# Eight projection tiles of layer 1 as plain F32 matmuls in a two-layer decoder trunk

## The chip, the cores and the metric

The kernel runs on one core of one Trainium2 chip. The metric is the device time of one execution in microseconds; of three runs the median was 1395.73 us (1391.5 to 1395.9). The engines are PE (TensorE: PE for matmuls, PEld for the weight loads beside them), DVE (VectorE), ACT (ScalarE), POOL (GpSimd) and SP (SyncE, from which the DMAs of this kernel are issued). Each engine works off its own instructions in a fixed order.

## The reference, cut to what matters

The input x has 512 tokens of width 1024, all in float32, and there are two layers. Each layer normalises x, multiplies it by one wide matrix `w_in`, and gives the columns of the product to three groups of heads: low-rank latent attention (cq, ckv, kr), sparse attention with an indexer that picks the 128 best keys of each query (aq, ak, av, qi, ki, wi), and retention (rq, rk, rv, rg).

```
for l in range(DEPTH):
    h = rmsnorm(x, g_mix[l])
    (cq, ckv, kr, aq, ak, av, qi, ki, wi, rq, rk, rv, rg) = jnp.split(h @ w_in[l], split_at, axis=-1)
    ...                       # three groups of heads
    x = x + jnp.concatenate([o_a, o_b, o_c], axis=-1) @ w_out[l]
    hf = rmsnorm(x, g_mlp[l])
    x = x + jnp.square(jax.nn.relu(hf @ w_ff1[l])) @ w_ff2[l]
return rmsnorm(x, g_final)
```

The change concerns the product `h @ w_in` of the first layer.

## The kernel before, in words

The activations lie transposed, features on the 128 partitions and the 512 tokens along a row, so x is eight tiles of 128x512. `w_in` is worked in tiles of 128 output columns: tile n (`win[l, n]`, 128x1024 in memory) holds the eight 128x128 blocks for the eight x tiles. Tile 0 feeds the latent key, 1 and 2 are the index queries qi0 and qi1, 3 and 4 the retention queries rq0 and rq1, 5 and 6 the retention keys rk0 and rk1, 7 and 8 the gates rg0 and rg1, 9 and 10 the sparse queries aq0 and aq1, 11 and 12 kv, 13 to 18 the latent queries cq0 to cq5. Columns that are needed with tokens on the partitions are worked apart ("tk", the token tiles, L677 to L707).

A product keeps float32 accuracy by halves. `make_u` (L281) writes x times the gain as a high half in fp32r and a low half, the difference. `wsplit` (L199) does the same with a weight tile: two 128x512 copies into `wh` (L187 on ACT, or L189 on POOL) and two subtractions into `wl` (L209 on DVE, or L211 on POOL). `product` (L215) then runs, for each of the eight blocks, `mm3` (L143): high by high, high by low, low by high, thus 24 fp32r matmuls of 128x512 for a tile. The norm's factor is applied to the product afterwards (`scaled`, L642).

Which engine makes the halves turns with a counter by `MHI = 'aaap'` and `MLO = 'vp'`: three copies in four on ACT, the subtractions in turn on DVE and POOL. Raw weight tiles have `WRB = 4` buffers (`wr`), halves `WB = 4` each. Tiles of the general pool `g` have 13 buffers.

The order of the tiles in a layer is written out in the string `ORDER`: after qi0, rg0, qi1 and the token tiles ("tk") it goes through rq0, rk0, rq1, rk1, rg1, aq1, aq0, kv0, kv1 and cq0 to cq5, with index scores ("ix", L715), top-k rounds ("t", L731) and retention scores ("r", L781) between. A list scheduler sets the place of every instruction on its engine, by the priorities in `PRI`; a top-k round has -225, so it fills what is left of DVE. A round finds the eight largest scores of a row (L734) and strikes them out (L735); there are 48 rounds in a layer, and three masks (L739) behind them.

A rotary tile (rq, rk, aq, qi) is scaled on DVE, its halves are swapped by two DMAs (L302), and the tables (L291, DMA) are multiplied in on POOL and DVE (L138); `rq_tile` (L759) then splits it and sends the halves by DMA into the `qk` tiles (L768, L769). Index scores go through a relu on ACT (L722) and are summed on DVE (L727). The retention scores multiply the `qk` tiles of rq and rk.

For the latent queries `factor` (L882) makes a norm factor out of summed squares: a chain of small DVE instructions from L247 to L887. `round_rope` (L952) and L976 apply it to the query products.

Of the kernel before, what the change touches and what calls it, by code (L numbers as in the profile page):

```python
# [11 lines left out]
FR = mybir.dt.float32r  # L12
BF = mybir.dt.bfloat16
AF = mybir.ActivationFunctionType
ALU = mybir.AluOpType
AX = mybir.AxisListType

P = 128
# [3 lines left out]
KD = 8  # L22
# [8 lines left out]
WRB = 4  # L31
# [24 lines left out]
MLO = 'vp'  # L56
ORDER = 'qi0 rg0 qi1 tk ix1 ix2 F rq0 ix3 rk0 rq1 r1 t2 r1 r1 t3 rk1 t4 rg1 aq1 r1 r1 aq0 F t2 t2 F F F F F t2 F F kv0 kv1 F F t1 F F r2 cq0 t2 t2 r1 r1 cq1 r4 kvf kvc t2 cq2 cq3 t5 r7 cq4 t1 t4 r16 t4 t2 cq5 r12 F F r6 r12 t1 F r2 v0 r16 r14 F r14 r9 cqf r2 t4 mk F t2 r1 r2 cqc r2 r2 r3 F t1 r11 rr0 t1 t4 t4 q0 r4 k1 t5 F k0 t2 r4 F t2 r2 q1 t4 r6 t4 r2 F t10 t10 t3 t4 m0 r2 r6 t2 r5 m1 r3 r2 r1 t3 t2 t5 a0 a1 t2 k2 t4 t4 dm t7 t4 r10 r1 t9 rr1 r1 t7 t3 r2 t4 a2 q2 a3 q3 t3 r3 m2 r7 t6 r10 r2 d2 t5 d3 d0 t15 d1 k3 t4 t2 r2 t2 t1 t3 m3 v1 a4 t8 t1 a6 F t3 r2 t4 t59 t2 r1 t6 r2 a7 r2 t3 t1 t3 a5 t2 t3 F r1 F r3 r2 r10 F r2 F'
PRI = {'fin': 0, 'w': 99, 'e': 59, 't': -225, 'rope': 0, 'split': 133, 'q': -16, 'qm': 0, 'rr': 0, 'v': 5, 'k': 0, 'att': 0, 'pv': 0, 'done': -70, 'ret': -44, 'st': 65, 'x': 0, 'tab': -20, 'cq': 0, 'tok': 15, 'idx': 0, 'dm': 8, 'rg': 0, 'km': 0, 'qi': 0, 'aq': 0}
TOPK = 128
NEG = -1e30  # L60
GONE = -3e38
# [4 lines left out]
G_MIX, G_MLP, G_Q, G_KV, G_RET, G_LAYER = 0, 8, 16, 22, 24, 26  # L66
# [5 lines left out]
def trunk_kernel(ctx, tc, xT, gains, win, wtk, wuq, wukv, wout, wff1, wff2, tabs, cf, cb, outT):  # L72
    nc = tc.nc
# [9 lines left out]
    def hp(k):  # L83
        return tc.high_priority(PRI[k]) if PRI[k] else nullcontext()

    def nm(s):
        count["n"] += 1
        return f"{s}_{count['n']}"

    def S(tag, bufs, shape=None, dt=F32):  # L90
        return sb.tile(shape or [P, T], dt, tag=tag, bufs=bufs, name=nm(tag))

    def g_(dt=F32, shape=None):
        return S("g", GB, shape, dt)
# [3 lines left out]
    def pair(tag, bufs, dt=FR):  # L98
        t = S(tag, bufs, [P, 2, T], dt)
        return t[:, 0], t[:, 1]  # L100

    def x_():
        if not spare:
            spare.extend(pair("x", 4, F32))
        return spare.pop(0)
# [16 lines left out]
    def tiny(w, tag="tiny", bufs=8, dt=F32):  # L122
        return sb.tile([P, w], dt, tag=tag, bufs=bufs, name=nm(tag))

    def mm_ps():
        return pp.tile([P, T], F32, tag="mm", bufs=3, name=nm("mm"))
# [13 lines left out]
    def mm(out, lhsT, rhs, start, stop):  # L140
        return nc.tensor.matmul(out, lhsT, rhs, start=start, stop=stop)  # L141

    def mm3(out, ah, al, bh, bl, start, stop):  # L143
        mm(out, ah, bh, start, False)
        mm(out, ah, bl, False, False)
        return mm(out, al, bh, False, stop)
# [12 lines left out]
    x = [x_() for k in range(KD)]  # L159
# [20 lines left out]
    def gcol(i):  # L180
        return gn[:, i : i + 1]
# [11 lines left out]
    def wchunk(src, width, parts=2):  # L193
        with hp("w"):
            raw = S("wr", WRB, [P, 1024])[:, :width]
            nc.sync.dma_start(raw, src)
            return wsplit(raw, width, parts)

    def wsplit(raw, width, parts):  # L199
        res = []  # L200
        w = width // parts
        for c in range(parts):
            hi, lo = S("wh", WB, None, FR)[:, :w], S("wl", WB, None, FR)[:, :w]
            rc = raw[:, c * w : (c + 1) * w]
            n = count["w"]
            count["w"] += 1
            copy_fr(hi, rc, H0[n] if n < len(H0) else mode["hi"][n % len(mode["hi"])])
            if (L0[n] if n < len(L0) else mode["lo"][n % len(mode["lo"])]) == "v":
                nc.vector.tensor_sub(lo, rc, R(hi))  # L209
            else:  # L210
                nc.gpsimd.tensor_sub(lo, rc, R(hi))  # L211
            res.append((hi, lo))
        return res

    def product(ch, kk, acts, cols=slice(0, T), out=None):  # L215
        out = mm_ps() if out is None else out
        per = len(kk) // len(ch)
        for j, k in enumerate(kk):
            ah, al = acts[k]
            h, l = ch[j // per]  # L220
            js = slice(j % per * P, j % per * P + P)
            order[j] = mm3(out[:, cols], h[:, js], l[:, js], ah[:, cols], al[:, cols], j == 0, j == len(kk) - 1)
        return out

    def gemm(wsrc, kk, acts, raw=None):
        parts = 2 if len(kk) > 2 else 1
        ch = wchunk(wsrc, len(kk) * P, parts) if raw is None else wsplit(raw, len(kk) * P, parts)
        return product(ch, kk, acts)
# [25 lines left out]
    def stats(ss, dim, r2=None):  # L254
        with hp("st"):
            ps = sc_ps()
            for b in range(NB):
                mm(ps[:, b : b + 1], ss[:, b * P : (b + 1) * P], ones, True, True)
            return rstd(ps[:, :4], dim, r2)

    def bcast(y, out):
        with hp("st"):
            ps = sc_ps()
            for b in range(NB):
                nc.tensor.transpose(ps[:, b * P : (b + 1) * P], y[:, b : b + 1].to_broadcast([P, P]), ident)
            nc.scalar.activation(out, ps, AF.Copy)
# [11 lines left out]
    def after(key):  # L278
        return tc.issue_after(order[key].ins) if key in order else nullcontext()

    def make_u(xk, gc):  # L281
        uh, ul = u2()
        order["uh"] = nc.scalar.activation(uh, xk, AF.Copy, scale=gc)
        order["ul"] = nc.vector.scalar_tensor_tensor(ul, xk, gc, R(uh), op0=ALU.mult, op1=ALU.subtract)  # L284
        return uh, ul
# [29 lines left out]
    k8 = list(range(8))  # L315
# [292 lines left out]
    for l in range(DEPTH):  # L608
        G0 = l * G_LAYER
        mode.update(hi=MHI, lo=MLO)  # L610
        begun = {}
        if l == 0:
            u = [make_u(x[k], gcol(G0 + G_MIX + k)) for k in range(KD)]
            ss = S("ss", 1)
            for k in range(KD):
                s = g_() if k else ss
                if SQP[k] == "p":
                    nc.gpsimd.tensor_mul(s, x[k], x[k])
                else:
                    with after("uh"):  # L620
                        nc.scalar.activation(s, x[k], AF.Square)
                if k:
                    with after("ul"):
                        nc.vector.tensor_add(ss, ss, s)
            rtok = tiny(4, "rtok", 2)
            nc.vector.tensor_copy(rtok, stats(ss, 1024))
            rb = g_()
            bcast(rtok, rb)
        else:
            u, rtok, rb = nxt.u, nxt.rtok, nxt.rb  # L630
            for n in (0, 1):
                ch = wchunk(win[l, n], 1024)
                begun[n] = ch, product(ch, k8, u, early)
            nxt.finish(xp, late, sums)

        def win_tile(n, raw=None):
            if n in begun:
                ch, out = begun[n]
                return product(ch, k8, u, late, out)
            return gemm(win[l, n], k8, u, raw)  # L640

        def scaled(ps, z):  # L642
# [98 lines left out]

        for _ in range(TOPK // 8):
            for j in range(1, NB):
# [15 lines left out]
        def rq_tile(pr, base, tb):  # L759
            z = rope(scaled(win_tile(base + pr), zz_()), table(tb + pr), odd)  # L760
            a = qk_()
            lows = (x_() if base == 3 else g_()).bitcast(FR)
            if RD[base == 3] == "d":
                hi = g_(FR)
                split(z, hi, lows)
                for e in range(2):
                    own, other = slice(64 * e, 64 * e + 64), slice(64 - 64 * e, 128 - 64 * e)
                    nc.sync.dma_start(R(a[own, e]), R(hi[own]))  # L768
                    nc.sync.dma_start(R(a[other, e]), R((hi if base == 3 else lows)[own]))  # L769
            else:  # L770
                for e in range(2):
                    own, other = slice(64 * e, 64 * e + 64), slice(64 - 64 * e, 128 - 64 * e)
                    nc.scalar.activation(a[own, e], z[own], AF.Copy)
                    if base == 3:
                        nc.vector.tensor_sub(lows[own], z[own], R(a[own, e]))
                        nc.sync.dma_start(R(a[other, e]), R(a[own, e]))
                    else:
                        nc.vector.tensor_sub(a[other, e], z[own], R(a[own, e]))
            rqk[base, pr] = a, lows
# [380 lines left out]
        for step in ORDER.split():  # L1160
            name, num = step.rstrip("0123456789"), step[len(step.rstrip("0123456789")) :]
            n = int(num or 0)
# [55 lines left out]
        x = [xp[n // 2][:, n % 2] for n in range(KD)]  # L1218
# [132 lines left out]
```

## Time and profile before

| | |
|---|---|
| median of three runs | 1395.73 us (1391.5 to 1395.9) |
| the profiled execution | 1398.68 us, span 1396.9 us |
| mean granted clock of PE | 0.976 |
| PE busy | 1326.8 us, 95% of the span |
| DVE busy | 1103.2 us, 79% |
| ACT busy | 666.2 us, 48% |
| POOL busy | 331.6 us, 24% |

The span is the time from the first to the last instruction of the profiled execution; 1.8 us of its time lie around it. Times in rows are microseconds from the span's start, unless marked ns. PEclk is the share of full speed that PE was granted. A wait stands in square brackets with the instruction that ended it.

### The profile page before, as it was taken

To read this page: it belongs to the slowest core of one execution; us is meant where nothing else is said; L and a number is where in the kernel's file an instruction comes from. 1 tells how busy PE (TensorE), PEld (TensorE's weight loads), DVE (VectorE), ACT (ScalarE), POOL (GpSimd) and SP (SyncE) were. 2 spreads that over 40 slices of the span, in tenths; PEclk is the share of its full clock that TensorE was granted. 3 is DMA by queue.
4 is the path that set the end of the run, shared out by engine and by line. 5 is a ranking of instruction groups with operands and counts; after the bars stand their busy time and mean duration, and the time that the engine had idled before them with its cause. 6 is when DMAs were issued, how large, how long until landed. Compare 5 with 4: busy or idle time off the path is not lost. (4 is left out here: it accounts for less than half of the span.)

```text
span 1396.9 us, 20211 instructions
## 1 busy us (share of the span) xinstructions
PE 1326.8 (95%) x7304; PEld 1102.9 (79%) x7304; DVE 1103.2 (79%) x1843; ACT 666.2 (48%) x1179; POOL 331.6 (24%) x337
## 2 busy tenths in 40 slices
PE   7889988989999999999999999898999999999997
PEld 5767775757788888899988777566778888888997
DVE  6789998887677767788658999878767776777875
ACT  3343443676344344455535345357844444445652
POOL 4446752424100000000034666334240000000000
PEclk9999999999999999999999999999999999999998
DMA  6457522302355554556546671231035555554652
GB/s 218 99 162 183 157 64 70 113 16 63 123 192 171 183 174 154 180 180 215 178 143 188 192 181 52 77 100 46 16 121 163 164 179 178 161 180 151 209 184 78
DMA packets 75780, 197.56 MB, mean 141 GB/s; under 512 B 8960, under 2 KB 13792, under 8 KB 75680
## 3 DMA queue, kind: packets, MB, share of 16 engines
q1 hardware_dynamic: 74528, 195.22, 45.6%
q8 instruction: 58, 0.95, 0.3%
q10 hardware_dynamic: 1152, 1.05, 0.2%
q14 instruction: 42, 0.34, 0.1%
HBM read 155.68 MB, written 20.97 MB: 126 GB/s over the span
## 5 line engine op out<-in xcount | busy, mean ns | idle before, releaser
L141 PE MATMUL mm<-u,wh 128*128 128x512 f32 (+1 forms) x1776 | 561.5, 396 | 1.6 <-DVE u L284 1.2
L141 PEld LDWEIGHTS mm<-u,wh 128*128 128x128 f32 x1776 | 332.7, 190 | 77.4 <-DVE u L284 2.6
L141 PE MATMUL mm<-u,wl 128*128 128x512 f32 (+1 forms) x888 | 351.0, 395 | 3.9 <-DVE wl L209 3.9
L187 ACT ACTIVATE wh<-wr 128x512 fp32r<-128x512 f32 (+2 forms) x247 | 149.8, 611 | 315.8 <-PE mm L141 197.3
L209 DVE TENSOR_TENSOR wl<-wr,wh 128x512 fp32r<-128x512 f32 (+2 forms) x208 | 153.5, 739 | 89.6 <-ACT wh L187 87.3
L211 POOL TENSOR_TENSOR wl<-wr,wh 128x512 fp32r<-128x512 f32 (+2 forms) x80 | 104.7, 1309 | 443.3 <-ACT wh L187 423.7
L141 PEld LDWEIGHTS mm<-u,wl 128*128 128x128 f32 x888 | 168.8, 190 | 43.4 <-DVE wl L209 4.8
L489 DVE TENSOR_TENSOR u<-wr,u 128x1024 fp32r<-128x1024 f32 x54 | 65.8, 1221 | 25.1 <-ACT u L488 24.7
L141 PE MATMUL o<-p,v 128*128 128x512 f32 (+2 forms) x316 | 83.4, 370 | 1.8 <-POOL p L138 1.3
L488 ACT ACTIVATE u<-wr 128x1024 fp32r<-128x1024 f32 x54 | 57.1, 1058 | 53.3 <-PE o L502 14.0
L431 DVE TENSOR_TENSOR sm<-wr 128x512 f32<-128x512 f32 x64 | 44.5, 695 | 36.3 <-DMA wr<-in_wff 36.3
L502 PEld LDWEIGHTS sc<-g,v 128*128 128x128 f32 x576 | 70.3, 188 | 2.9
L502 PE MATMUL sc<-g,v 128*128 128x256 f32 x576 | 71.0, 277 | 0.0
L141 PEld LDWEIGHTS o<-p,v 128*128 128x128 f32 x316 | 52.4, 198 | 12.8 <-DVE p L138 4.1
L419 DVE SCALAR_TENSOR_TENSOR g<-mm,g 128x512 f32<-128x512 f32 x64 | 44.1, 688 | 23.0 <-PE mm L141 22.8
L138 DVE TENSOR_TENSOR p<-pe,p 128x512 fp32r<-128x512 f32 (+2 forms) x78 | 46.5, 623 | 12.0 <-POOL p L189 9.9
L189 POOL TENSOR_SCALAR p<-pe 128x512 fp32r<-128x512 f32 (+1 forms) x46 | 35.1, 767 | 74.2 <-ACT pe L1082 72.6
L735 DVE MATCH_REPLACE8 g<-m,g 128x512 f32<-128x512 f32 (+2 forms) x96 | 51.4, 539 | 0.0
L734 DVE MAX8 m<-g 128x8 f32<-128x256 f32 (+2 forms) x96 | 50.3, 547 | 0.2
L435 ACT ACTIVATE v<-wr 128x1024 fp32r<-128x1024 f32 x32 | 34.1, 1066 | 33.3 <-DVE wr L433 33.1
L189 POOL TENSOR_SCALAR wh<-wr 128x512 fp32r<-128x512 f32 (+3 forms) x41 | 29.8, 726 | 82.9 <-PE mm L141 57.6
L141 PE MATMUL sc<-u,qk 97*128 97x512 f32 (+5 forms) x192 | 46.7, 358 | 2.4 <-ACT pe L1082 2.4
(299 smaller groups left out, 2742.0 us busy)
## 6 DMA issues: line engine op xcount, KB each, us to landing
wr<-in_wff SPq DMA_DIRECT2D x160, 512.0 KB
wr<-in_win SPq DMA_DIRECT2D x37, 512.0 KB
ws<-sm SPq DMA_DIRECT2D x32, 512.0 KB
wr<-ws SPq DMA_DIRECT2D x32, 512.0 KB
tab<-in_tabs SPq DMA_DIRECT2D x20, 512.0 KB
wr<-in_wout SPq DMA_DIRECT2D x16, 512.0 KB
p<-p SPq DMA_DIRECT2D x40, 128.0 KB
wr<-in_wuq SPq DMA_DIRECT2D x12, 384.0 KB
```

The costliest lines, as they stand in the source:

```text
L138: (nc.vector if eng == "v" else nc.gpsimd).tensor_tensor(out, a, b, op=op)
L141: return nc.tensor.matmul(out, lhsT, rhs, start=start, stop=stop)
L187: nc.scalar.activation(out, src, AF.Copy)
L189: nc.gpsimd.tensor_scalar(out, src, 1.0, 1.0, op0=ALU.mult, op1=ALU.mult)
L209: nc.vector.tensor_sub(lo, rc, R(hi))
L211: nc.gpsimd.tensor_sub(lo, rc, R(hi))
L431: nc.vector.tensor_add(sm[:, h], w[0], w[1])
L488: nc.scalar.activation(wh, t, AF.Copy)
L489: nc.vector.tensor_sub(wl, t, R(wh))
L502: nc.tensor.matmul(outs[m][0], a[:, m * P : m * P + P], b, start=i == 0 and outs[m][1] and n == 0, stop=i == KP - 1 and n == 2, skip_group ...
L734: nc.vector.max(m8, accs[j])
L735: nc.vector.match_replace(out=accs[j], in_to_replace=m8, in_values=accs[j], imm_value=GONE)
```

## The change

`WHOLE` names the tiles 2, 3, 4, 5, 6, 8, 9 and 10 (qi1, rq0, rq1, rk0, rk1, rg1, aq0, aq1). In layer 1 `win_tile` no longer splits these: the raw weights go straight to PE, as F32, against x times its gain, also F32, in eight matmuls instead of 24. For that x is multiplied by its gain in place on POOL (eight new instructions, behind the squares that are taken of x). Since x now lives until the last of these tiles, the low half of rq is taken from the pool `g` in layer 1 instead of from the x buffers. Layer 2 is computed as before.

```
+WHOLE = (2, 3, 4, 5, 6, 8, 9, 10)
...
-        begun = {}
+        begun, xs = {}, x
...
+            for k in range(KD):
+                nc.gpsimd.tensor_scalar(x[k], x[k], gcol(G0 + G_MIX + k), 1.0, op0=ALU.mult, op1=ALU.mult)
...
             if n in begun:
                 ch, out = begun[n]
                 return product(ch, k8, u, late, out)
+            if l == 0 and n in WHOLE:
+                raw, out = S("wr", WRB, [P, 1024]), mm_ps()
+                with hp("w"):
+                    nc.sync.dma_start(raw, win[l, n])
+                for k in k8:
+                    mm(out, raw[:, k * P : k * P + P], xs[k], k == 0, k == KD - 1)
+                return out
             return gemm(win[l, n], k8, u, raw)
...
-            lows = (x_() if base == 3 else g_()).bitcast(FR)
+            lows = (x_() if base == 3 and l else g_()).bitcast(FR)
```

The scheduler places the rest of layer 1 anew; lines behind L628 have numbers higher by 3 to 10. Over the whole program PE goes from 5578 to 5486 rows of instructions, DVE from 1715 to 1707, ACT from 1173 to 1161, POOL from 334 to 328 and SP from 514 to 516. Three places follow, each first before, then after.

On SP, around the first rotary table of the retention tiles (`tab_725` before, `tab_685` after; `p_723` and `p_683` are rq0's product, `wr` raw weights, `v` the index queries, `km` the latent key). Before:

```order
L668 DMA v_322<-g_411 32x4x384
L669 DMA v_322<-g_412 32x4x384
L670 DMA v_322<-g_411 32x4x384
L196 DMA wr_836<-in_win 128x1024
L302 DMA p_723<-p_723 64x512 x2
L291 DMA tab_725<-in_tabs 128x1024
```

After:

```order
L303 DMA p_257<-p_257 16x512 x4
L303 DMA p_319<-p_319 64x512 x2
L646 DMA wr_672<-in_win 128x1024
L292 DMA tab_685<-in_tabs 128x1024
L660 DMA km_272<-km_270 64x512
L661 DMA km_272<-km_271 64x512
```

The table of rq0 stood behind the swap of rq0 itself; it now stands ahead of the latent key's copies, sixteen rows before that swap.

On PE, at the first retention scores (`sc_888` and those after it before, `sc_801` and on after; `qk` are the retention queries and keys, `mm` a projection tile). Before:

```order
L141 MATMUL mm_1045<-u_146,wh_1037 128x512 x2
L141 MATMUL mm_1045<-u_146,wl_1038 128x512
L141 MATMUL sc_888<-qk_732,qk_827 128x512
L141 MATMUL sc_888<-x_733,qk_827 128x512
L141 MATMUL sc_901<-qk_732,qk_827 128x384
L141 MATMUL sc_901<-x_733,qk_827 128x384
L141 MATMUL sc_908<-qk_732,qk_827 128x256
```

After:

```order
L142 MATMUL mm_838<-x_110,wr_837 128x512 x2
L142 MATMUL mm_879<-x_107,wr_878 128x512 x2
L142 MATMUL sc_801<-qk_692,qk_763 128x512
L142 MATMUL sc_801<-g_693,qk_763 128x512
L142 MATMUL sc_814<-qk_692,qk_763 128x384
L142 MATMUL sc_814<-g_693,qk_763 128x384
L142 MATMUL sc_821<-qk_692,qk_763 128x256
```

The scores stood in the sixth tile behind the token tiles (aq1, `mm_1045`); they now stand in the fifth (rg1, `mm_879`), behind two of its eight matmuls.

On DVE, around the query factor of the latent attention (L247 to L887 before, L248 to L897 after; `m` and L734/L735 or L744/L745 are top-k rounds, `ma` and L749 the masks, `wl` low halves of other weights). Before, from the row behind L247 on:

```order
L734 MAX m_422_1835<-g_604 128x8
L734 MAX m_423_1838<-g_646 128x8
L249 TENSOR_SCALAR tiny_1816<-tiny_1816 128x4
L734 MAX m_424_1841<-g_741 128x8
L236 TENSOR_TENSOR tiny_1822<-tiny_1817 128x4
L819 SCALAR_TENSOR_TENSOR g_1743<-sc_1745,g_1743 128x512
L237 SCALAR_TENSOR_TENSOR tiny_1822<-tiny_1822,tiny_1816 128x4
L232 TENSOR_TENSOR qk_1848<-mm_1975,qk_1847 64x512
L238 SCALAR_TENSOR_TENSOR tiny_1817<-tiny_1822,tiny_1817 128x4
L735 MATCH_REPLACE g_646<-m_423_1838,g_646 128x384
L209 TENSOR_TENSOR wl_2010<-wr_2003,wh_2009 128x384
L887 TENSOR_TENSOR tiny_1826<-tiny_1817,rtok_193 128x4
```

After:

```order
L749 TENSOR_SCALAR ma_415_1739<-g_630 128x384
L749 TENSOR_SCALAR ma_416_1741<-g_701 128x512
L210 TENSOR_TENSOR wl_1806<-wr_1803,wh_1805 128x256
L248 SCALAR_TENSOR_TENSOR tiny_1633<-sc_1628,tiny_1626 128x4
L250 TENSOR_SCALAR tiny_1633<-tiny_1633 128x4
L237 TENSOR_TENSOR tiny_1639<-tiny_1634 128x4
L238 SCALAR_TENSOR_TENSOR tiny_1639<-tiny_1639,tiny_1633 128x4
L239 SCALAR_TENSOR_TENSOR tiny_1634<-tiny_1639,tiny_1634 128x4
L829 SCALAR_TENSOR_TENSOR g_1560<-sc_1562,g_1560 128x512
L897 TENSOR_TENSOR tiny_1643<-tiny_1634,rtok_201 128x4
```

Before, top-k rounds stand between the factor's steps, and go on behind them; after, the last round and the masks are done ahead of it. Counted along DVE, 78 of the 96 halves of rounds stand ahead of the factor before, all 96 and the three masks after; ahead of the first cq tile's L878 (L888 after) it is 32 before and 53 after.

## Rows read from the trace of the kernel before

**Rows 1.** the page: busy us, share of the span, instructions.

```profile
PE 1326.8 (95%) x7304; PEld 1102.9 (79%) x7304; DVE 1103.2 (79%) x1843; ACT 666.2 (48%) x1179; POOL 331.6 (24%) x337
```

**Rows 2.** windows: length, busy us (instructions) by engine, PEclk, DMA share, GB/s.

```profile
57.00:123.00 66.00, 56.47 (x215) 42.65 (x213) 59.92 (x107) 26.39 (x60) 30.24 (x28) 0.90 0.55 149
75.00:143.00 68.00, 61.88 (x238) 46.57 (x237) 64.48 (x107) 26.06 (x52) 38.68 (x36) 0.92 0.65 169
140.00:180.00 40.00, 39.71 (x172) 29.91 (x172) 39.14 (x89) 19.25 (x37) 30.38 (x30) 1.00 0.51 139
195.00:215.00 20.00, 13.87 (x60) 10.32 (x59) 18.97 (x36) 7.70 (x17) 13.21 (x15) 0.97 0.32 95
```

**Rows 3.** timeline of PE, split tile: start, length, instruction, [idle before].

```profile
153.22 0.63 PE L141 MATMUL mm<-u,wh 128*128 128x512 f32 x2
...
153.92 0.63 PE L141 MATMUL mm<-u,wh 128*128 128x512 f32 x2
```

**Rows 4.** timeline of PE, plain F32 matmul and what follows it.

```profile
193.24 1.02 PE L141 MATMUL sc<-g,cft 128*128 128x512 f32 x2
194.09 0.95 PE L141 MATMUL sc<-ones,ss 128*128 128x1 f32 x8
```

**Rows 5.** groups by form, 0 to 180 us: busy us, mean ns, idle.

```profile
L211 POOL TENSOR_TENSOR wl<-wr,wh 128x512 fp32r<-128x512 f32 x19 | 27.9, 1471 | 10.5 <-ACT wh L187 9.6
L209 DVE TENSOR_TENSOR wl<-wr,wh 128x512 fp32r<-128x512 f32 x20 | 20.2, 1014 | 3.8 <-ACT wh L187 3.6
L187 ACT ACTIVATE wh<-wr 128x512 fp32r<-128x512 f32 x29 | 17.6, 626 | 24.2 <-DMA wr<-in_win 13.3 <-PE mm L141 10.7
...
L189 POOL TENSOR_SCALAR wh<-wr 128x512 fp32r<-128x512 f32 x10 | 9.4, 941 | 13.9 <-DMA wr<-in_win 8.3 <-issue 4.3 <-PE mm L141 1.3
```

**Rows 6.** timeline of PE, tile rq0 and the first index scores.

```profile
59.95 0.71 PE L141 MATMUL mm<-u,wl 128*128 128x512 f32 x1 [1.98 <-DVE wl L209]
60.46 1.05 PE L141 MATMUL mm<-u,wh 128*128 128x512 f32 x2
...
61.74 1.05 PE L141 MATMUL mm<-u,wh 128*128 128x512 f32 x2
...
65.62 0.38 PE L141 MATMUL sc<-g,v 96*128 96x256 f32 x1 [1.64 <-ACT g L722]
```

**Rows 7.** timeline of PE, later index scores, retention scores.

```profile
84.44 0.80 PE L141 MATMUL sc<-g,v 96*128 96x512 f32 x1 [3.39 <-ACT g L722]
...
102.83 0.49 PE L141 MATMUL sc<-qk,qk 128*128 128x512 f32 x1 [1.40 <-DMA qk<-g]
...
105.45 1.22 PE L141 MATMUL mm<-u,wh 128*128 128x512 f32 x2
...
111.46 0.39 PE L141 MATMUL mm<-u,wl 128*128 128x512 f32 x1
```

**Rows 8.** timelines of ACT and POOL, rope of rq0.

```profile
83.27 0.63 ACT L187 ACTIVATE g<-p 128x512 fp32r<-128x512 f32 x1 [4.16 <-DVE p L138]
...
75.62 1.49 POOL L138 TENSOR_TENSOR p<-p,tab 128x512 f32<-128x512 f32 x1 [12.21 <-DMA tab<-in_tabs]
```

**Rows 9.** the page, costliest groups: a top-k round on DVE.

```profile
L735 DVE MATCH_REPLACE8 g<-m,g 128x512 f32<-128x512 f32 (+2 forms) x96 | 51.4, 539 | 0.0
L734 DVE MAX8 m<-g 128x8 f32<-128x256 f32 (+2 forms) x96 | 50.3, 547 | 0.2
```

**Rows 10.** timeline of DVE, query factor (L247 to L887) and L976.

```profile
195.08 0.16 DVE L247 SCALAR_TENSOR_TENSOR tiny<-sc,tiny 128x4 f32<-128x4 f32 x1
...
201.27 0.15 DVE L887 TENSOR_TENSOR tiny<-tiny,rtok 128x4 f32<-128x4 f32 x1
...
214.06 1.29 DVE L976 TENSOR_TENSOR g<-mm,g 128x512 f32<-128x512 f32 x2
```

**Rows 11.** timeline of PE, the waits on L887 and L976.

```profile
201.47 0.65 PE L265 MATMUL sc<-cft,tiny 128*128 128x128 f32 x4 [1.20 <-DVE tiny L887]
...
214.89 1.19 PE L141 MATMUL mm<-x,wh 128*128 128x512 f32 x2 [4.93 <-DVE g L976]
```

## The prediction

> **What bounds the kernel now.** I read the page's busy shares first, then windows over the stretch that the change touches, then PE's timeline there with the waits in brackets, and last the timelines of DVE, ACT and POOL at those waits. PE is busy 1326.8 us of the span, DVE 1103.2 [rows 1]. An average over two layers says little about eight tiles of the first, so the windows come next. From 57 to 123 us, where seven of the eight tiles lie, PE is busy 56.47 of 66 us at a granted clock of 0.90: 9.5 us are waits. From 140 to 180 us it is busy 39.71 of 40 at full clock, and DVE 39.14: both are full. From 195 to 215 us PE does 13.87 of 20, DVE 18.97 [rows 2]. So PE has holes in two places, one ahead of the full stretch and one behind it, and DVE is nearly full from 75 us on (64.48 of 68).
>
> The holes of the first place have names. In rq0 PE waits 1.98 us for a low half (L209), then 1.64 us for a relu on ACT [rows 6], later 3.39 us for another relu, and 1.40 us for the DMA that brings the retention operands [rows 7]. After a wait the granted clock falls from 2.4 to 1.2 GHz for a while: a group of three matmuls takes 61.74 - 60.46 = 1.28 us [rows 6] where it takes 153.92 - 153.22 = 0.70 at full clock [rows 3], so each group loses 0.58. The second place is the query factor: PE waits 1.20 us for L887 and 4.93 us for L976 [rows 11], while DVE goes from L247 at 195.08 by way of L887 at 201.27 to L976 at 214.06 [rows 10].
>
> **Part 1, the matmuls: a cost.** A split tile is eight groups of 0.70 us [rows 3], 5.6 us. A plain F32 matmul of the same 128x512 shape stands once in that window: two records from 193.24, and the next operation starts at 194.09, so one costs 0.85 us [rows 4]. Eight make 6.8, and with rounding up to 0.86 I take 6.88: +1.28 a tile, +10.2 us for eight. PE has no cover for it: a matmul is on PE's path wherever PE is the late one. One tile (qi1) lies before 57 us, +1.3; seven lie in the first place, +9.0.
>
> The price may be a matter of where it was read, since the row shows one F32 matmul alone. The Trainium skill, "FP8 and Floating Point Precision", section "TensorE Precision Notes", says that true FP32 takes four passes through the array. Four of the passes that the split tile makes in 0.233 us each would be 0.93 us, eight 7.47, and the change would then cost PE +1.87 a tile, +15.0 us in all. The row's 0.85 us is the lower of the two, and the sum goes by the row.
>
> **Part 2, the halves: they leave three engines.** Sixteen copies (12 on ACT at 0.63 us, 4 on POOL at 0.94) and sixteen subtractions (8 on DVE at 1.01, 8 on POOL at 1.47) go [rows 5]: 7.5 us of ACT, 8.1 of DVE, 15.5 of POOL. POOL gets eight scalings of x, bounded by its 128x512 tensor_scalar at 0.94 us [rows 5], 7.5 us; they lie between the squares and the first rotary tables, where POOL has gaps, and nothing before qi1's tile asks for them. If that cover were gone, qi1 would be late by some of these 7.5 us; I take 0. What counts is which wait on PE these instructions ended. The first, 1.98 us on a low half, has no source left: gone. The 1.64 us on the relu behind it came from ACT standing for the token tiles, which on DVE stood behind two such subtractions of 2 x 1.01 us: gone.
>
> The 3.39 us on the later relu goes for another reason. ACT stood 4.16 us for rq0's rope (L138 on DVE) ahead of that relu, and the rope was late because POOL waited 12.21 us for its table [rows 8]. The table now stands on SP ahead of rq0's swap, not behind it, and it no longer waits there for the product of rq0. So rq0's rope is done well before the relus that follow it. Behind the first of these waits and behind the 3.39 us one, about 2.5 groups ran at half clock, 1.4 us each time. Gone in all: 1.98 + 1.64 + 3.39 + 2 x 1.4 = 9.8 us against +9.0.
>
> The retention scores come one tile earlier. Their wait for the `qk` DMAs is 1.40 us now, and from 105.45 to 111.46 the tiles ran at half clock [rows 7], 2.7 us lost. rk0's operands will be ready earlier by the rope and the shorter queue, the scores ask earlier by a tile: the ends are 4.1 us gained and, if the DMA lands where it did, a wait of one more tile, 6.9 us lost. I take half of the gain, 2.1, since rq0's and rk0's tables were the delay.
>
> Sum for the first place: +9.0 - 9.8 - 2.1 = -2.9 us. Ends: +9.0 with every wait replaced, -4.9 with the four waits (8.4 us) and all half-clock groups (5.5) gone.
>
> **Part 3, DVE's order: a gain behind the full stretch.** A half of a top-k round costs 0.54 to 0.55 us [rows 9]. Before, 78 halves stand ahead of L247 and 88 ahead of L976, so ten halves, 5.5 us, lie inside the chain for which PE waits 1.20 and 4.93 us [rows 11]. After, none does. That is the upper end: -5.5, and up to 1.4 more if the half clock behind the wait goes too. But the ten were moved, not dropped. Up to L976 DVE has 8 halves (4.4 us) and three masks (at most a half each, 1.6) more than before, and 8 subtractions (8.1) less: 2.1 us less work. If DVE is full all the way, only these 2.1 us arrive at L976. If DVE is late by the whole extra work ahead of L247, nothing is gained: 0 is the other end. DVE was busy 18.97 of the 20 us [rows 2], so I take a value between 2.1 and 5.5 that is nearer to the former: -3.5.
>
> **Part 4, the rest.** The low half of rq in `g` instead of x, and raw weights that hold their buffer until PE is done with the tile: four raw tiles are prefetched, over 25 us of PE at 6.88 each, so I cost them at 0; if a `g` buffer comes late to the kv conversion it is a matter of a wait of the 1 to 2 us seen above. Layer 2 is untouched.
>
> **Sum.** +1.3 - 2.9 - 3.5 = -5.1 us against the profiled execution's own 1398.68 (span 1396.9 and 1.8 around it): 1393.6. The median of the runs lies 0.21% below that execution, so on its scale the forecast is 1390.6 us.
>
> **Rivals.** (a) *DVE becomes the bound in the full stretch: slower.* Ahead of the first cq tile's evacuation 21 more halves stand on DVE, 11.5 us, and seven subtractions fewer, 7.1 us: +4.4 where DVE has 3.5 us idle in 68 [rows 2] and PE waits for nothing from 140 to 180. It decides if DVE falls behind by more than the product buffers cover; PE then stands for evacuations and for low halves. Against it: three product buffers, each a tile of 5.6 us. With the relu waits half replaced (first place +4.0), +4.4 here and -3.5 in the factor: +1.3 + 4.0 + 4.4 - 3.5 = +6.2, 1404.9 on the profile, 1401.9 on the median's scale.
> (b) *The tiles balance, and the factor's wait stays.* DVE is as late at L976 as now, since its work was moved and not dropped; the sum is +1.3 - 2.9 = -1.6, 1394.1. For it: DVE's 18.97 of 20 us. Against: the chain itself loses ten instructions.
> (c) *Every wait goes.* First place -4.9, factor -5.5 - 1.4: +1.3 - 4.9 - 6.9 = -10.5, 1385.2. For it: all four waits of the first place hang on instructions that leave or move up. Against: the retention operands still come by DMA.
> (d) *An F32 matmul is dearer than the row.* Four of the 0.233 us of an fp32r matmul (0.70 / 3) make 0.93; the eight tiles then cost 4.8 us more than I count: -0.3, 1395.4. This is what the four passes of the Trainium skill ("FP8 and Floating Point Precision", "TensorE Precision Notes") would make here. Against it: the one matmul in the trace took 0.85.
> (e) *The F32 tiles run at 1.2 GHz.* 64 matmuls would cost some 55 us more. Against it: the one in the trace ran at full clock beside split tiles.
>
> **How the numbers follow.** Chances: forecast 0.42 (its own range 1387.5 to 1393.5), (a) 0.22, (b) 0.17, (c) 0.12, (d) 0.05, (e) 0.02. Against no change, 0.3% of the time is 4.2 us, about what a measurement of this kernel can tell: 1391.5 and below is faster. Of the forecast three quarters (0.32) lie there and 0.10 within; (c) is faster; (b) and (d) are within; of (a) 0.20 is slower and 0.02 within; (e) is slower. That makes faster 0.44, same 0.34, slower 0.22. The range reaches over (c) by the spread of the runs, 1383, and up to (a), 1402.
>
> **What would show it.** The F32 tiles' records should stand 0.85 to 0.86 us a matmul at granted clock 1.0, 6.9 us a tile. PE should have no wait on L732 above 1 us between 57 and 123 us, POOL none on rq0's table, and the retention scores a wait of 0 to 2 us. L248 to L897 should take about 3 to 4 us instead of 6.2, and PE should wait under 3 us for L986. I am wrong if PE shows new waits between 110 and 185 us, on low halves or evacuations that stand behind top-k rounds, or if an F32 matmul takes 0.9 us or more.

## The result, and the profile after

The changed kernel took 1405.25 us (median of 12 runs, 1398.0 to 1410.38) against 1395.82 us before (12 runs, 1391.5 to 1398.0). The ratio is 1.0061 with a 95% interval of 1.0042 to 1.0081: slower by 0.6% (the two medians alone give 1.0068), where 1390.6 was forecast, and above the range's upper end of 1402. The profiled execution has a span of 1403.1 us, 6.2 more than before.

The page of the changed kernel, its engines (busy us, share, instructions), against [rows 1]:

```profile
PE 1338.9 (95%) x7238; PEld 1092.2 (78%) x7240; DVE 1089.4 (78%) x1835; ACT 659.9 (47%) x1167; POOL 319.4 (23%) x333
```

PE is 12.1 us busier, and DVE, ACT and POOL are less busy, as intended. The windows, with the columns of [rows 2] (length, busy us and instructions of PE, PEld, DVE, ACT, POOL, then PEclk, DMA share, GB/s), of the changed kernel:

```profile
57.00:123.00 66.00, 63.99 (x181) 32.74 (x180) 58.23 (x130) 24.27 (x55) 19.45 (x21) 1.00 0.67 181
140.00:180.00 40.00, 37.61 (x173) 29.08 (x171) 39.80 (x94) 19.49 (x37) 28.93 (x28) 1.00 0.18 54
215.00:230.00 15.00, 15.00 (x89) 11.16 (x87) 10.90 (x20) 7.18 (x18) 3.78 (x5) 1.00 0.34 112
230.00:260.00 30.00, 29.93 (x109) 17.98 (x110) 18.18 (x29) 10.50 (x24) 8.63 (x11) 0.72 0.15 44
```

and the last two of them in the kernel before:

```profile
215.00:230.00 15.00, 15.00 (x67) 10.54 (x67) 11.73 (x23) 4.24 (x9) 1.01 (x1) 0.82 0.20 63
230.00:260.00 30.00, 29.97 (x144) 19.73 (x144) 24.19 (x47) 16.17 (x35) 10.39 (x14) 1.00 0.34 111
```

From 57 to 123 us PE is now busy 63.99 of 66 us at a granted clock of 1.00; it was 56.47 at 0.90. There lies the gain. From 230 to 260 us PE is busy 29.93 of 30 us (29.97 before), but the granted clock is 0.72 where it was 1.00. A busy share alone does not show this loss; the clock beside it does. At most 30 x 0.28 = 8.4 us are lost there; it is less where an instruction does not take twice as long at half clock. From 215 to 230 us the changed kernel is ahead (1.00 against 0.82).

The same instruction in both traces says where the lead goes. Times are starts in us from the span's start:

| what PE starts | before | after | after - before |
|---|---|---|---|
| sum of squares for the kv factor | 159.68 | 154.04 | -5.6 |
| sum of squares for the query factor | 194.09 | 190.99 | -3.1 |
| transposition of the second pair's maximum (L1012, L1022) | 229.48 | 222.65 | -6.8 |
| transposition of the sparse maximum (L1104, L1114) | 255.12 | 250.73 | -4.4 |
| norm before layer 1's MLP | 365.45 | 367.06 | +1.6 |
| sum of squares for layer 2's kv factor | 836.07 | 839.30 | +3.2 |
| norm before layer 2's MLP | 1045.53 | 1051.20 | +5.7 |

Up to 223 us the change gains 6.8 us. From there to the MLP it loses 8.4; the fall of the clock between 230 and 260 us accounts for most of it (the run first8 below puts it at 6.5). The order differs there, so the sparse row itself compares unlike amounts of work done. Layer 2, whose instructions stand in the same order in both kernels, adds 4 more.

The place is `dsa_max`, which takes the row maximum of the sparse attention's scores: sixteen matmuls `sc<-km,qk` that contract over 64 partitions, each followed by a bf16 matmul that adds the mask. The timeline of PE in the changed kernel:

```profile
229.67 0.38 PE L142 MATMUL sc<-km,qk 64*128 64x256 f32 x1
229.99 0.28 PE L142 MATMUL sc<-cbt 128*128 128x256 bf16 x1
230.20 0.38 PE L142 MATMUL sc<-km,qk 64*128 64x256 f32 x1
...
232.83 0.57 PE L142 MATMUL sc<-km,qk 64*128 64x256 f32 x1
233.33 0.39 PE L142 MATMUL sc<-ma,cbt 128*128 128x256 bf16 x1
233.65 0.58 PE L142 MATMUL sc<-km,qk 64*128 64x256 f32 x1
...
250.04 0.62 PE L142 MATMUL mm<-x,wh 128*128 128x512 f32 x2
...
250.73 0.27 PE L1114 MATMUL sc<-cft,mt 128*16 128x128 f32 x1
```

From 229.67 to 230.20 one score and its mask take 0.53 us; from 232.83 to 233.65 the same pair takes 0.82. Nothing waits: the clock has fallen, and it comes back only at 250 us. Eight of these pairs stand here one behind the other; the first six run at full clock, and the fall meets the seventh. In the kernel before the first of them is at 236.51, six run bare, and value and projection matmuls stand between the rest:

```profile
236.51 0.38 PE L141 MATMUL sc<-km,qk 64*128 64x256 f32 x1
...
239.49 1.06 PE L141 MATMUL o<-p,v 128*128 128x512 f32 x4
...
243.69 0.40 PE L141 MATMUL mm<-u,wh 128*128 128x512 f32 x1
...
245.41 0.63 PE L141 MATMUL mm<-x,wh 128*128 128x512 f32 x2
...
255.12 0.27 PE L1104 MATMUL sc<-cft,mt 128*16 128x128 f32 x1
```

Why the order differs is read from the order, not shown by a run of its own: before, the masks came late on DVE (L739 at 230.33 and 244.03 us), and the scheduler set other matmuls between the scores. With the rounds finished ahead of the query factor the masks are ready, and by this reading the scores close ranks.

### The profile page after: what moved, and what is told of

It is laid out like the page before. It is cut to its first block, busy times and chain, and to the rows that moved or that the text cites. A ratio compares the mean times of both kernels' runs of the same rounds, so it can differ in the third digit from the quotient of the medians.

```text
span 1403.1 us, 20066 instructions
## 1 busy us (share of the span) xinstructions
PE 1338.9 (95%) x7238; PEld 1092.2 (78%) x7240; DVE 1089.4 (78%) x1835; ACT 659.9 (47%) x1167; POOL 319.4 (23%) x333
## 5 line engine op out<-in xcount | busy, mean ns | idle before, releaser
L142 PE MATMUL mm<-u,wh 128*128 128x512 f32 (+1 forms) x1648 | 517.1, 394 | 2.0 <-DVE u L285 2.0
L142 PEld LDWEIGHTS mm<-u,wh 128*128 128x128 f32 x1648 | 306.5, 189 | 72.0 <-DVE u L285 3.9
L142 PE MATMUL mm<-u,wl 128*128 128x512 f32 (+1 forms) x824 | 324.8, 394 | 1.3 <-DVE wl L210 1.3
L188 ACT ACTIVATE wh<-wr 128x512 fp32r<-128x512 f32 (+2 forms) x235 | 143.0, 610 | 314.3 <-PE mm L142 204.7
L210 DVE TENSOR_TENSOR wl<-wr,wh 128x512 fp32r<-128x512 f32 (+2 forms) x200 | 144.6, 724 | 84.5 <-ACT wh L188 83.9
L212 POOL TENSOR_TENSOR wl<-wr,wh 128x512 fp32r<-128x512 f32 (+2 forms) x72 | 89.9, 1249 | 430.3 <-ACT wh L188 404.9
L142 PEld LDWEIGHTS mm<-u,wl 128*128 128x128 f32 x824 | 156.1, 189 | 37.2 <-DVE wl L210 1.7
L142 PE MATMUL o<-p,v 128*128 128x512 f32 (+2 forms) x316 | 87.9, 382 | 4.5 <-DVE p L139 2.0
L139 DVE TENSOR_TENSOR p<-pe,p 128x512 fp32r<-128x512 f32 (+2 forms) x78 | 47.3, 634 | 13.2 <-POOL p L190 11.2
L142 PE MATMUL mm<-x,wr 128*128 128x512 f32 x128 | 57.3, 593 | 0.0
L745 DVE MATCH_REPLACE8 g<-m,g 128x256 f32<-128x256 f32 (+2 forms) x96 | 51.3, 538 | 0.0
L744 DVE MAX8 m<-g 128x8 f32<-128x256 f32 (+2 forms) x96 | 50.3, 545 | 0.2
```

The lines of the kernel that those rows point to most:

```text
L139: (nc.vector if eng == "v" else nc.gpsimd).tensor_tensor(out, a, b, op=op)
L188: nc.scalar.activation(out, src, AF.Copy)
L744: nc.vector.max(m8, accs[j])
L745: nc.vector.match_replace(out=accs[j], in_to_replace=m8, in_values=accs[j], imm_value=GONE)
```

## The experiments

Twelve runs follow: ten new kernels, and two of the kernels a second time for another profile. Ratios are to the kernel before on the same chip, with 95% intervals; where two ratios are divided, the two kernels ran on different chips.

**One operand, the order untouched.** `kmd` holds the high and low halves of the key in its 128 partitions, and `dq[..][0]` the query twice, so the maximum can be taken of a full-row product with the same instructions in the same places:

```
-mm(o, dq[h // 2][0][0:64, h % 2, j * P : (j + 1) * P], kmh[0:64, :n], True, False)
+kr, kk = (slice(0, 64), kmh) if l else (slice(0, P), kmd)
+mm(o, dq[h // 2][0][kr, h % 2, j * P : (j + 1) * P], kk[kr, :n], True, False)
```

> The changed kernel with one operand changed: in layer 1 the scores from which the sparse attention takes its row maximum (dsa_max) contract over 128 partitions (both halves of the key against the doubled query) instead of 64. The order of all instructions on all engines is that of the changed kernel. Theory A (the clock): the changed kernel gains until 217 us and then loses some 8.5 us because its 64-row scores stand nearly back to back from 229.7 us on and the granted clock falls to 1.2 GHz from 232.8 to 249.9; with 128 rows the clock stays at 2.4 GHz from 225 to 250 us and the median is about 1397 (ratio to before 1.000). Theory B (F32 is too dear): the eight tiles cost PE more than the waits give back, the clock there is a bystander: 1405, ratio 1.006.

Measured: 1392.12 us, ratio 0.9957 (0.994 to 0.9974). PE's timeline and windows in this kernel:

```profile
229.12 0.27 PE L142 MATMUL sc<-km,qk 128*128 128x256 f32 x1
229.24 0.28 PE L142 MATMUL sc<-cbt 128*128 128x256 bf16 x1
229.28 0.36 PE L142 MATMUL sc<-km,qk 128*128 128x256 f32 x1
...
229.52 0.37 PE L142 MATMUL sc<-km,qk 128*128 128x256 f32 x1
...
239.24 0.28 PE L1115 MATMUL sc<-cft,mt 128*16 128x128 f32 x1
```

```profile
215.00:230.00 15.00, 15.00 (x92) 11.37 (x91) 10.86 (x20) 7.65 (x18) 3.79 (x5) 1.00 0.27 87
230.00:260.00 30.00, 28.43 (x168) 21.27 (x167) 27.59 (x44) 18.00 (x38) 13.20 (x18) 1.00 0.29 94
```

The clock stays at 1.00. A pair takes 0.245 us (229.28 to 229.52; 0.525 with 64 rows), and the stretch to the transposition takes 10.1 us instead of 21.1. So a part of this gain is not the clock: a 64-row score costs more even at full clock. The next kernels separate the two. The same eight F32 tiles, in the same order, now beat the kernel before, which theory B did not allow; but since full rows gain at full clock too, it falls for certain only with the next kernel.

**The order, the operands untouched.** The priority of `dsa_max` is lowered in layer 1:

```
-PRI = {... 'dm': 8, ...}
+PRI = {... 'dm': 8, 'dm0': -40, ...}
-with hp("dm"):
+with hp("dm" if l else "dm0"):
```

> The changed kernel with the priority of dsa_max lowered in layer 1, so that the scheduler sets projection and value matmuls between its 64-row scores, as in the kernel before. Theory A: the clock stays up from 225 to 250 us for most of the time, median 1395 to 1400. Theory B: 1405, whatever stands between the scores.

Measured: 1394.84 us, ratio 0.9985 (0.9966 to 1.0004). The window:

```profile
230.00:260.00 30.00, 29.82 (x153) 20.37 (x154) 23.85 (x42) 16.27 (x33) 11.18 (x16) 1.00 0.36 115
```

Same scores, same 64 rows, other matmuls between them: clock 1.00, and 0.76% less time than the changed kernel (0.9985 / 1.0061; 0.5 to 1.0%). That is theory A without any help from faster scores.

**Full rows in the first eight scores alone** (`if l or j > 1` in the edit above):

> The changed kernel with 128-row operands for the first eight of layer 1's sixteen dsa_max scores alone (the two of 256 keys for each head, which stand one behind the other with nothing but masks between); the other eight keep 64 rows. The order is that of the changed kernel. If the bare run of the first scores brings the clock down (theory A, narrow), it stays at 2.4 GHz from 229 to 250 us: 1393 to 1396, ratio 0.997 to 1.000. If 64-row scores lower it wherever they are dense, it falls some 3 us later, in the scores of 384 and 512 keys: 1398 to 1403. Theory B: 1405.

Measured: 1394.37 us, ratio 0.9994 (0.9976 to 1.0013). PE's timeline and window:

```profile
229.38 0.27 PE L142 MATMUL sc<-km,qk 128*128 128x256 f32 x1
...
231.57 0.36 PE L142 MATMUL sc<-km,qk 128*128 128x256 f32 x1
...
232.46 0.44 PE L142 MATMUL sc<-km,qk 64*128 64x384 f32 x1
232.83 0.34 PE L142 MATMUL sc<-ma,cbt 128*128 128x384 bf16 x1
...
241.71 0.28 PE L1115 MATMUL sc<-cft,mt 128*16 128x128 f32 x1
```

```profile
230.00:260.00 30.00, 28.40 (x151) 19.57 (x151) 25.38 (x42) 15.69 (x33) 11.32 (x16) 1.00 0.29 89
```

The other eight scores keep 64 rows and run at full clock. The stretch takes 241.71 - 229.38 = 12.3 us, 8.7 less than in the changed kernel. At full clock a 64-row pair costs 0.525 us here and a full-row pair 0.245 (229.28 to 229.52 in the kernel above), so eight of them are worth 2.2 us; the other 6.5 are the clock. So in the changed kernel's layer 1 it is the bare run of the first eight that brings the clock down.

**The changed kernel again.**

> The changed kernel again, for a second profile. Theory A: the half-clock stretch of some 17 us in layer 1's sparse scores is there again, PEclk between 230 and 260 us about 0.7, ratio 1.004 to 1.008. If it was an accident of one execution, the clock is 1.0 there.

Measured: 1406.54 us, ratio 1.0070 (1.0044 to 1.0096), and the second profile has the same window:

```profile
230.00:260.00 30.00, 29.93 (x110) 18.52 (x111) 18.44 (x31) 10.55 (x23) 8.61 (x11) 0.72 0.19 59
```

Both profiles have the fall, so it is not an accident of one execution. The mean granted clock of each run supports this: it averages 0.976 and 0.973 over the changed kernel's two sets (12 and 7 runs), and 0.981 to 0.982 over those of spread, first8 and rows128. A difference of 0.005 to 0.009 of 1400 us is 7 to 13 us. The changed kernel's two fastest runs of the first set (1398.0 and 1399.28 us) stand at 0.980 and 0.981, so the fall may be missing in some executions.

**Full rows in the kernel before.**

> The kernel before, all tiles split, with the 128-row operands in layer 1's dsa_max. It separates what full rows give by themselves from what they give back to the changed kernel: a 64-row score and its mask take 0.525 us in the changed kernel at full clock, a 128-row pair 0.245, so 28 pairs are worth up to 7.8 us where nothing else fills PE. Theory A (the changed kernel lost to the clock, which the kernel before kept): full rows are worth clearly less here than the 13 us they gave the changed kernel, 1391 to 1395 (ratio 0.996 to 0.999), and the eight F32 tiles then come out 0 to 6 us ahead. Theory B (full rows help both alike and the F32 tiles cost 9 us): 1384, ratio 0.991.

Measured: 1395.99 us, ratio 0.9983 (0.9964 to 1.0002). There are sixteen scores in a layer, not the 28 that the expectation counted, so full rows could give 4.5 us; they gave about 2.4, which is within noise. The changed kernel gained 1.0% (0.8 to 1.3%, 1.0061 / 0.9957) by the same edit. With full rows in both, the change stands at 0.9957 / 0.9983 = 0.9974 (0.995 to 1.000, the two half-widths combined as squares): about 0.3% faster, with an interval that reaches to no change and also holds the forecast's 0.9963.

**The side edits alone.** `WHOLE = ()` keeps the scaling of x and the low half of rq in the general pool:

> The changed kernel with an empty list of whole tiles: the scaling of x on POOL and the low half of rq in the general pool stay, all tiles are split as before. Theories A and B both expect the time of before, 1396, ratio 1.000 within 0.002, and no half-clock stretch in the sparse scores. A third theory C (the side edits cost something: the general pool or POOL's queue): 1400 or more.

Measured: 1402.72 us (10 runs, 1395.14 to 1408.65), ratio 1.0039 (1.0021 to 1.0057). By its time theory C was right, against both others; what makes the price, it does not show. Four more runs look into that:

> No whole tiles, but the side edits (x scaled on POOL, low half of rq in the general pool), and 128-row operands in layer 1's dsa_max. The side edits alone came out 5 us slower than before. If that is the clock in the sparse scores too, full rows remove it and this stands with the kernel before plus full rows, within 2 us. If the side edits cost by themselves (theory C), it stands 4 to 6 us above that kernel.

Measured: 1397.92 us, ratio 1.0005 (0.9986 to 1.0023), 0.22% (3 us) above the kernel before with full rows; the two intervals overlap, and the value lies between what was expected of the clock and what was expected of theory C.

> The side edits alone once more, for a second profile: its runs lay at 1395 to 1409 and the profile before was the fastest of them. Theory A expects in a slower execution a half-clock stretch that the first profile does not have; theory C the same clock and longer waits in the first 130 us.

Measured: one run of 1399.25 us, span 1397.5. Both profiles of this kernel have PEclk 1.00 from 230 to 260 us. But both are of executions faster than its median of 1402.72 (the first, 1395.14, is the fastest of its ten), so a fall in the sparse scores of the slower ones is not excluded. Over the ten runs the mean granted clock averages 0.976, against 0.978 in the kernel before on the same chip: some 3 of the 5 us are clock, and no trace shows in which stretch.

> No whole tiles and no scaling of x; only the low half of rq comes from the general pool in layer 1. The two side edits together came out at 1.0039. If the general pool is the price, 1.002 to 1.005; if it is POOL's scalings, 0.999 to 1.001.

> No whole tiles and the low half of rq from the x buffers as before; only the eight scalings of x on POOL are added, everything else in the order of before. If they are the price of the side edits, 1.002 to 1.005; if the general pool is, 0.999 to 1.001.

Measured: 1397.84 us, ratio 1.0016 (0.9997 to 1.0034), and 1398.93 us, 1.0016 (0.9998 to 1.0034). Neither can be told from no change. Together the side edits cost 0.39% with 64 rows, clear of noise, and 0.22% with full rows, not clear of it; which of them, and where, stays open.

Against the side edits alone the eight F32 tiles by themselves, with full rows in both (rows128 and none128), give 0.9957 / 1.0005 = 0.9952 (0.993 to 0.998), some 6.7 us.

**Bare scores in the kernel before.** The masks in layer 1's `dsa_max` are replaced by zeros and its priority is raised:

> The kernel before, all tiles split, with the masks in layer 1's dsa_max replaced by a zero mask (the row maximum is then taken over unselected keys too) and its priority raised, so that its 64-row scores stand without projection matmuls between them, earlier than the masks would allow. Theory A: the granted clock falls in those scores, some 3 to 8 us lost there against before. Theory B: within 2 us of before, clock up.

Measured: 1399.46 us, ratio 1.0012 (0.9992 to 1.0031), and no fall of the clock:

```profile
230.00:260.00 30.00, 29.59 (x149) 20.87 (x149) 24.23 (x45) 15.23 (x33) 9.63 (x14) 1.00 0.23 73
```

The expectation of theory A failed here. The edit did not make the order of the changed kernel: four scores stand bare, then attention matmuls, then five more. So this kernel does not test theory A.

Layer 2 has the test that the edit missed. There eight such scores stand one behind the other, with nothing but masks between, in every kernel but both128, the one before included. The window around them in the kernel before, then in rows128, whose layer 2 keeps 64 rows and the same order:

```profile
910.00:950.00 40.00, 39.58 (x195) 27.45 (x194) 31.96 (x56) 21.82 (x45) 12.74 (x19) 0.91 0.31 102
910.00:950.00 40.00, 39.17 (x211) 27.55 (x211) 34.60 (x57) 22.62 (x45) 17.43 (x23) 1.00 0.30 99
```

The kernel before loses its clock behind them, and rows128 does not. Of the thirteen profiles with 64 rows in layer 2, eight show the fall between 905 and 930 us, and five (rows128, b128, bunch40, none_look and lows_only) show full clock throughout that stretch. Such a run can thus be followed by a fall and need not be, and what decides is not shown. A single profile at full clock proves little; for layer 1 the weight lies on the times and mean clocks of all runs.

**A faster version.** The changed kernel with full rows in both layers:

> The changed kernel with 128-row operands in dsa_max of both layers. Layer 2's order is that of before, and its clock there is 0.9 between 900 and 950 us. Theory A: a further 2 to 6 us, 1387 to 1390, ratio 0.991 to 0.995. If full rows matter only where the scores stand bare of other matmuls: as with layer 1 alone, 0.9957.

Measured: 1387.12 us (6 runs), ratio 0.9925 (0.9897 to 0.9954): faster than both kernels, and 0.3% below rows128, with an interval that reaches to no change.

## Why the prediction was wrong

**The matmuls: right.** The changed kernel's PE, tiles rq0, rk0 and rk1 to rg1 (each F32 matmul leaves two records):

```profile
57.57 5.32 PE L142 MATMUL mm<-x,wr 128*128 128x512 f32 x12
62.32 0.68 PE L142 MATMUL sc<-g,v 96*128 96x256 f32 x1
62.84 7.03 PE L142 MATMUL mm<-x,wr 128*128 128x512 f32 x16
69.31 0.92 PE L142 MATMUL sc<-g,v 96*128 96x256 f32 x3
...
80.46 10.46 PE L142 MATMUL mm<-x,wr 128*128 128x512 f32 x24
91.51 0.47 PE L142 MATMUL sc<-qk,qk 128*128 128x512 f32 x1 [0.58 <-issue]
```

From 62.84 to 69.31 us eight matmuls run, 0.81 each; from 80.46 to 90.93 (91.51 less the wait) twelve, 0.87 each. Forecast: 0.86. Over the five long runs of these tiles it is 0.83, which makes some 1.9 us less for 64 matmuls. Four times 0.233, as rival (d) had it, would be 0.93; the trace stays below it.

**The waits of the first place: right, and better than forecast.** None of the four is left above 0.58 us, and no group at half clock. ACT finds rq0's rope ready:

```profile
75.76 0.62 ACT L188 ACTIVATE g<-p 128x512 fp32r<-128x512 f32 x1
```

No wait stands there; it was 4.16 us [rows 8]. By 154 us the gain is 5.6 us where -1.6 was forecast for the two terms together (+1.3 - 2.9): the retention wait and its half-clock groups went nearly whole, not by half, and the matmuls were cheaper than 0.86.

**The factor chain: right in itself, mis-sized as a net gain.** DVE and PE of the changed kernel:

```profile
191.98 0.16 DVE L248 SCALAR_TENSOR_TENSOR tiny<-sc,tiny 128x4 f32<-128x4 f32 x1 [0.95 <-PE sc L142]
...
195.88 0.15 DVE L897 TENSOR_TENSOR tiny<-tiny,rtok 128x4 f32<-128x4 f32 x1
...
209.53 1.29 DVE L986 TENSOR_TENSOR g<-mm,g 128x512 f32<-128x512 f32 x2
```

```profile
196.08 0.65 PE L266 MATMUL sc<-cft,tiny 128*128 128x128 f32 x4 [1.00 <-DVE tiny L897]
...
210.36 0.70 PE L142 MATMUL mm<-x,wh 128*128 128x512 f32 x2 [2.72 <-DVE g L986]
```

L248 to L897 takes 3.9 us instead of 6.2, and the wait for L986 is 2.72 instead of 4.93 [rows 11]. From the query factor to the second pair's maximum the lead grows from -3.1 to -6.8, by 3.7 us. But 2.5 us of lead were spent before it: between 140 and 180 us PE is busy 37.61 of 40, where it was 39.71. PE's two longest waits ahead of the query factor:

```profile
180.43 0.39 PE L142 MATMUL mm<-wh,g 128*128 128x256 f32 x1 [2.14 <-ACT g L274]
...
182.33 0.58 PE L142 MATMUL mm<-wh,g 128*128 128x256 f32 x1 [0.93 <-DVE v L960]
```

ACT's L274 had itself waited 3.29 us for L888 on DVE, which takes a product out of its buffer and stood behind halves of top-k rounds (177.04 to 178.94 us). This is rival (a), in small, and the sign of being wrong that the prediction named. Net, from -5.6 to -6.8, this term gave 1.2 us, not 3.5. The sum of the three terms was forecast at -5.1 and measured at -6.8. It comes out near by luck: the first place gave 4.0 us more, and this one 2.3 us less.

**The step that failed is part 4, "the rest".** It put the rest of the program at 0, and so took for granted that behind the factor nothing changes but waits. The order showed three masks moved ahead of the factor; the prediction counted them as DVE's work and did not ask what PE's scheduler would do with scores whose masks are ready. It put eight 64-row scores together, and the granted clock went to 1.2 GHz for 17 us with PE busy all the time. That took back 6.5 us in the stretch itself (first8); by the ratios of the changed kernel and spread it is 10.7 us (0.76%), though there the order differs too. No rival had it: (e) had the lower clock in the F32 tiles, where it did not fall.

Part 4 also costed the side edits at 0, and they took 5 us (none) or 3 (none128, within noise). And it called layer 2 untouched: its instructions are, but the changed kernel loses 4.1 us more there. On the profile's scale the miss of 11.5 us (1405.1 against 1393.6) is thus -1.7 in the three terms, +8.4 between 223 us and the MLP, +4.1 in layer 2 and +0.7 behind it. The clock in layer 1 is not the whole of it: where it did not fall, the change stands at 0.9985 (spread) and 0.9994 (first8), and 0.9963 was forecast.

**What stays open.** In layer 2 the changed kernel's first index scores wait longer, with the same order of instructions. One of them after, then before:

```profile
753.26 0.38 PE L142 MATMUL sc<-g,v 96*128 96x256 f32 x1 [2.77 <-ACT g L732]
```

```profile
749.22 0.39 PE L141 MATMUL sc<-g,v 96*128 96x256 f32 x1 [0.19 <-ACT g L722]
```

From the last sum of squares of layer 2's first norm (711.69 us before, 713.79 after) to that for its kv factor the kernel before takes 124.4 us, the changed kernel 125.5 and 125.3 in its two profiles, first8 123.0 and spread 128.5, all with one order there. One L139 on DVE, 0.69 us before, takes 1.62 in the changed kernel, where a subtraction on POOL runs beside all of its first part (745.67 to 746.96 us); that the one stretches the other is not shown. A further part of the 4.1 us is the clock behind layer 2's eight scores: 0.87 from 910 to 950 us, against 0.91 before. Why one execution meets more of this than another was not settled.

## What to carry to other kernels

Read the granted clock beside PE's busy share, and do it where the order is changed at all, not where the edit is. When data become ready earlier, ask what the scheduler will now put side by side: matmuls over 64 of the 128 partitions, with nothing but their masks between them, can be followed by half clock on a PE that never waits. If the operands allow it, contract such scores over all 128 partitions; it cost no instruction here.

## What was not expected of the hardware

Matmuls over 64 partitions between full ones cost more at full clock too: a score of 256 columns and its mask took 0.525 us, with 128 partitions 0.245. In the changed kernel the clock fell at the seventh of eight such pairs in a row, with PE busy throughout, and stayed at half for 17 us, through value and projection matmuls of full height (232.83 to 250.04). The fall is not bound to the order: behind the eight pairs of layer 2 it came in eight of thirteen profiles, the kernel before's among them.
